# Products of depth 64 in pairs on the two halves of the array's rows

## The chip, the cores and the metric

One core of a Trainium2 chip runs the whole kernel as one program. The core has TensorE (PE in the rows; its weight loads are PEld), VectorE (DVE), ScalarE (ACT), GpSimd (POOL) and SyncE (SP), each with its own queue of instructions taken in order, and 16 DMA engines. The metric is the device time of the program in microseconds (us), median of three runs. Beside it stands one profiled execution, whose trace is read below.

## The reference

One encoder layer for 512 tokens of width 1024, in fp32: a mixer, a cross-attention into 256 memory tokens, a mixture of 64 experts (top 8 of them per token) with a shared expert, and a layer norm behind each. The change lies in the mixer. Its first group of heads is a sparse attention whose keys an indexer selects, its second a differential attention. What matters of it:

```python
# indexer: 8 heads of depth 64, one key of depth 64 for all heads, a weight per head and query
rel = jax.nn.relu(jnp.einsum('bqhd,bsd->bqhs', qib, k_idx) * IDX_DIM ** -0.5)
iscore = jnp.einsum('bqh,bqhs->bqs', wib, rel)          # then top 128 keys of each query
# sparse attention: queries of depth 64 go up to the latent of depth 128
q_lat = jnp.einsum('bqhd,hcd->bqhc', qb, w_uk)
sc = jnp.einsum('bqhc,bqkc->bqhk', q_lat, c_sel) * scale
# differential attention: 4 heads, two maps of depth 64 each
s1 = jnp.einsum('bqhd,bshd->bhqs', q1b, k1) * scale + bias
s2 = jnp.einsum('bqhd,bshd->bhqs', q2b, k2) * scale + bias
attn = softmax(s1) - lam * softmax(s2)
```

## The kernel before

**Numbers.** A product in fp32 is made of three in a rounded format: each operand is split into a high part (a cast on ScalarE) and a low part (source minus high, on VectorE or GpSimd; helper `split`, lines 94 and 95), and `mm3` (lines 101 to 103) adds high x high, high x low and low x high into one bank of PSUM. There are eight banks of 512 columns, handed out in turn by `bank()`; 20 large buffers (`slot`), 6 small ones (`wk`).

**Stages.** The layer norm and transposes of x; then the input projections, one block of 128 columns after the other (three products for each of 8 slices of the depth, 24 in all); the indexer's scores and the selection of 128 keys; the differential heads; the sparse attention; the memory attention; the router; then the experts, whose weights (3 x 1 MB each) stream in from HBM.

**Order.** Each part is a generator (`head_scores`, `index_scores`, `select`, `latent_up`, `dense` and so on) that issues a few instructions and yields two numbers: the time that its step takes on TensorE, and how long the next step isn't due. `schedule` holds a clock of its own, runs the first generator of a fixed list that is due, and so writes the program order of all engines before anything runs. `dense`, last in the list, goes through the projections and fills what the others leave; it yields after 12 products.

**The products of depth 64.** They are made in three ways. The differential heads (line 498) take the two maps of a head one after the other: the queries and keys of map 1 lie in partitions 0 to 63, those of map 2 in 64 to 127, and each map is an `mm3` of depth 64 with a yield behind it. The indexer (line 357) has two heads in the 128 partitions of a query tile; its key tile `kz` is held twice, once with zeros in the lower half and once with zeros in the upper, so that a product of depth 128 picks out one head. The sparse attention's way up to the latent (line 601) does the same with weights: `ukz` has zeros beside each head's 64 rows.

**The head weights of the indexer** (8 columns, 64 to 71 of the indexer's block) have a split of their own (`ww`) and a product of their own behind the key product (line 328), 24 products with 8 columns of weights over 384 tokens. The result goes through `wit` (line 330), three small transposes (line 334) and `widx`.

Of the kernel before, what the change touches and what calls it, by code (L numbers as in the profile page):

```python
# [11 lines left out]
F32R = mybir.dt.float32r  # L12
# [46 lines left out]
def encoder_layer(  # L59
# [245 lines left out]
    KW, IX = {}, {}  # L305

    def index_split(raw):
        hl = chunks.tile([P, 2, KD, P], F32R, tag="whl", name="kw", bufs=2)
        for j in range(2):
            js = slice(j * 64, (j + 1) * 64)  # L310
            split(hl[:, 0, :, js], hl[:, 1, :, js], raw[:, :, 0:64], lo_eng=nc.vector if j else nc.gpsimd)
        ww = wk([P, 2, KD, 8], F32R, name="ww")
        split(ww[:, 0], ww[:, 1], raw[:, :, 64:72])
        KW[0] = ww
        return hl

    def index_keys(wh, wl):
        ps = bank()
        yield from proj(ps, wh, wl, xt)
        kz = slot([P, 2, 2, SEQ], F32R, name="kz")  # L320
        IX["kz"] = kz
        fill0(kz[64:128, :, 0, :])
        fill0(kz[0:64, :, 1, :])
        for v in range(2):
            r = slice(64 * v, 64 * v + 64)
            split(kz[r, 0, v, :], kz[r, 1, v, :], ps[r, :])
        psw = bank()
        yield from proj(psw[0:8, 0:384], KW[0][:, 0], KW[0][:, 1], xt, P, SEQ)
        wit = wk([P, 384], name="wit")
        nc.scalar.activation(wit[0:8, :], psw[0:8, 0:384], AF.Copy, scale=float(A_HEADS) ** -0.5)  # L330
        yield 0.0, 0.0
        psw = bank()
        for i in range(3):
            nc.tensor.transpose(psw[:, i * 8:(i + 1) * 8], wit[0:8, i * P:(i + 1) * P], ident[0:8, 0:8])
# [13 lines left out]
    def index_scores():  # L348
        yield from wait("qi3")
        kz, qih, qil, widx = IX["kz"], IX[0], IX[1], IX["w"]  # L350
        for i in range(1, NT):
            w = (i + 1) * P
            isc = dsel[:, i - 1, :]
            q0 = (i - 1) * P
            for h in range(8):
                ps = bank()
                mm3(ps[:, 0:w], qih[:, h // 2, q0:q0 + P], qil[:, h // 2, q0:q0 + P],
                    kz[:, 0, h % 2, 0:w], kz[:, 1, h % 2, 0:w], True, True)
# [8 lines left out]
                yield 3 * w / 2400, w / 1500  # L367
# [118 lines left out]
    def head_scores():  # L486
        for h in range(B_HEADS):
# [47 lines left out]
    def latent_w():  # L535
        yield from wait("hs2")
        UW["uv"] = slot([P, 2, A_HEADS, P], F32R, name="uvz")
        UW["uk"] = slot([P, 2, A_HEADS, P], F32R, name="ukz")
        uvz, ukz = UW["uv"], UW["uk"]
# [4 lines left out]
        ukz_p = ukz.rearrange("p l (a v) c -> p l a v c", v=2)  # L544
# [5 lines left out]
        for l in range(2):  # L550
            fill0(ukz_p[64:128, l, :, 0, :])
            fill0(ukz_p[0:64, l, :, 1, :])
            fill0(uvz_p[:, l, :, 0, 64:128])
            fill0(uvz_p[:, l, :, 1, 0:64])
        yield 0.5, 1.0
        for v in range(2):
            r = slice(64 * v, 64 * v + 64)
            split(ukz_p[r, 0, :, v, :], ukz_p[r, 1, :, v, :], ps[r, :, :])
# [29 lines left out]
    def latent_up(u):  # L588

        us = slice(u * 256, (u + 1) * 256)  # L590
        for g in range(2):
            QL[u, g] = slot([P, 4, 2, 256], F32R, name="ql")
            for a in (2 * g, 2 * g + 1):
# [4 lines left out]
                for v in range(2):  # L598
                    h = 2 * a + v
                    ps = bank()  # L600
                    mm3(ps[:, 0:256], UW["uk"][:, 0, h, :], UW["uk"][:, 1, h, :], qa[:, 0, :], qa[:, 1, :], True, True)
                    split(QL[u, g][:, h % 4, 0, :], QL[u, g][:, h % 4, 1, :], ps[:, 0:256], scale=0.125 * 2.0 ** (h + 1))
                    yield 0.35, 0.2
# [1098 lines left out]
```

## Time and profile before

| | us |
|---|---|
| median of 3 runs (1312.59 to 1316.73) | 1313.4 |
| profiled execution, device time | 1301.79 |
| its span, first to last instruction | 1300.0 |
| TensorE busy, of the span | 1150.2 (88%) |
| weight loads busy | 907.3 (70%) |
| VectorE / ScalarE / GpSimd busy | 749.3 / 562.0 / 451.6 |

The profiled execution is one run; durations are read from it. Busy time is the union of an engine's instructions; matmuls overlap each other in the pipeline, so what one costs is the step from its start to the next one's start and not its duration. In the rows below, L12 is a line of the kernel, "out<-in" names the tiles, and a shape such as 64*128 64x512 is weights of 64 rows by 128 columns and a moving operand of 64 rows by 512 columns. An idle time names what ended it.

### The profile page before, as it was taken

How to read it: one execution, taken by the hardware profiler on the slowest of the kernel's cores; microseconds unless marked ns; L12 is line 12 of the kernel's file. 1: busy time of each engine (PE TensorE's matmuls, PEld its weight loads, DVE VectorE, ACT ScalarE, POOL GpSimd, SP SyncE). 2: the span in 40 equal slices, each digit the busy share in tenths (PEclk: the TensorE clock that was granted, in tenths of full speed). 3: DMA queues.
4: the chain of work that ended last, by engine and by line, in shares of the span. 5: the costliest groups of instructions: out<-in, count | busy, mean ns of one | idle time of the engine just before them, and what ended most of it. 6: DMA issues, size and time to landing. Idle time of an engine off the chain costs nothing. (4 is left out here: it accounts for less than half of the span.)

```text
span 1300.0 us, 20964 instructions
## 1 busy us (share of the span) xinstructions
PE 1150.2 (88%) x7768; PEld 907.3 (70%) x7768; DVE 749.3 (58%) x1602; ACT 562.0 (43%) x1006; POOL 451.6 (35%) x335
## 2 busy tenths in 40 slices
PE   2999999999898899879999999999879988898860
PEld 2887778998798798878877778777657544554320
DVE  7258986556865657787867777766456321311114
ACT  3235446654454443334645565555345112312122
POOL 4333444552236353461323322423222222222223
PEclk9999999999999899999999999999989998899895
DMA  7322134463426155688999999999999999999974
GB/s 224 82 81 65 49 99 117 123 206 122 130 65 211 50 175 204 229 306 301 294 316 332 349 327 356 339 355 360 349 331 342 342 345 377 380 360 363 356 272 141
DMA packets 136807, 319.37 MB, mean 246 GB/s; under 512 B 13296, under 2 KB 96240, under 8 KB 111872
## 3 DMA queue, kind: packets, MB, share of 16 engines
q1 hardware_dynamic: 119984, 275.83, 58.5%
q0 software_dynamic: 13632, 41.50, 13.7%
q8 instruction: 62, 1.02, 0.3%
q10 hardware_dynamic: 3088, 0.69, 0.3%
q14 instruction: 41, 0.34, 0.1%
HBM read 288.10 MB, written 35.19 MB: 249 GB/s over the span
## 5 line engine op out<-in xcount | busy, mean ns | idle before, releaser
L95 POOL TENSOR_TENSOR whl<-wraw,whl 128x1024 fp32r<-128x1024 f32 x81 | 195.6, 2416 | 265.4 <-ACT whl L94 239.4
L1357 POOL DMA_INDIRECT acc<-y,sidx x66 | 106.6, 1615 | 381.4 <-DMA acc<-y,sidx 205.9
L1269 DVE TENSOR_TENSOR whl<-wraw,whl 128x1024 fp32r<-128x1024 f32 x152 | 183.0, 1231 | 80.6 <-ACT whl L1268 80.0
L101 PE MATMUL ps<-whl,xt 128*96 128x256 f32 (+4 forms) x640 | 184.6, 288 | 3.9 <-ACT whl L1268 3.9
L102 PE MATMUL ps<-whl,xt 128*96 128x256 f32 (+4 forms) x640 | 179.8, 281 | 0.3 <-DVE whl L1269 0.3
L103 PE MATMUL ps<-whl,xt 128*96 128x256 f32 (+4 forms) x640 | 179.7, 281 | 0.0
L1268 ACT CAST whl<-wraw 128x1024 fp32r<-128x1024 f32 x152 | 152.3, 1054 | 25.3 <-DMA acc<-y,sidx 12.9
L1352 PE MATMUL ps<-wd,ht 128*96 128x512 f32 (+4 forms) x320 | 146.8, 602 | 3.2 <-DVE ht L1340 2.5
L1305 PE MATMUL ps<-wraw,xn 128*64 128x256 f32 (+1 forms) x832 | 114.8, 400 | 19.6 <-DMA wraw<-in_e_w_up_dram 7.7
L1324 ACT ACTIVATE sg<-ps 64x256 f32<-64x256 f32 (+6 forms) x66 | 25.0, 379 | 239.7 <-PE ps L1305 123.7
L94 ACT CAST whl<-wraw 128x1024 fp32r<-128x1024 f32 x91 | 95.4, 1048 | 57.5 <-PE ps L103 46.6
L1244 POOL DMA_INDIRECT xg<-rows,sidx x66 | 79.6, 1206 | 108.3 <-PE ps L1293 34.7
L101 PEld LDWEIGHTS ps<-whl,xt 128*96 128x96 f32 (+4 forms) x640 | 104.8, 164 | 4.6 <-ACT whl L1268 4.1
L102 PEld LDWEIGHTS ps<-whl,xt 128*96 128x96 f32 (+4 forms) x640 | 104.9, 164 | 0.7 <-DVE whl L1269 0.5
L103 PEld LDWEIGHTS ps<-whl,xt 128*96 128x96 f32 (+4 forms) x640 | 104.8, 164 | 0.3
L1305 PEld LDWEIGHTS ps<-wraw,xn 128*64 128x64 f32 (+1 forms) x832 | 60.0, 138 | 57.0 <-DMA wraw<-in_e_w_up_dram 9.7
L1352 PEld LDWEIGHTS ps<-wd,ht 128*96 128x96 f32 (+4 forms) x320 | 49.5, 163 | 71.2 <-issue 65.5
L1353 ACT COPY y<-ps 96x512 f32<-96x512 f32 (+4 forms) x80 | 46.4, 583 | 67.9 <-PE ps L1352 66.4
L1329 DVE SCALAR_TENSOR_TENSOR hm<-ps,og,sg 64x256 f32<-64x256 f32 (+4 forms) x54 | 36.8, 682 | 63.1 <-ACT sg L1324 51.0
L1340 DVE COPY ht<-ps 128x128 f32<-128x128 f32 (+6 forms) x66 | 21.5, 325 | 83.5 <-PE ps L1338 83.3
L101 PE MATMUL ps<-xTh,whl 128*128 128x512 f32 (+1 forms) x168 | 65.5, 390 | 0.0
L103 PE MATMUL ps<-xTh,whl 128*128 128x512 f32 (+1 forms) x168 | 63.8, 380 | 0.0
(421 smaller groups left out, 2763.4 us busy)
## 6 DMA issues: line engine op xcount, KB each, us to landing
wraw<-in_e_w_gate_dram SPq DMA_DIRECT2D x64, 1024.0 KB, 17.0
wraw<-in_e_w_up_dram SPq DMA_DIRECT2D x64, 1024.0 KB, 13.4
wd<-in_e_w_down_dram SPq DMA_DIRECT2D x64, 1024.0 KB, 13.3
wraw<-in_w_in_dram SPq DMA_DIRECT2D x21, 512.0 KB, 3.8
wraw<-in_m_wkv_dram SPq DMA_DIRECT2D x16, 512.0 KB, 4.4
wraw<-in_m_wq_dram SPq DMA_DIRECT2D x16, 512.0 KB, 4.0
wraw<-in_m_wo_dram SPq DMA_DIRECT2D x16, 512.0 KB, 3.5
wraw<-in_w_o_dram SPq DMA_DIRECT2D x12, 512.0 KB, 3.5
```

Of the source, the lines that this page charges most:

```text
L94: nc.scalar.copy(hi, src)
L95: eng.tensor_sub(lo, src, hi.bitcast(F32))
L101: nc.tensor.matmul(ps, lhsT=a, rhs=b, start=start, stop=False)
L102: nc.tensor.matmul(ps, lhsT=a, rhs=bl, start=False, stop=False)
L103: nc.tensor.matmul(ps, lhsT=al, rhs=b, start=False, stop=stop)
L1244: nc.gpsimd.indirect_dma_start(out=xg[0:n, :], out_offset=None, in_=rows, in_offset=bass.IndirectOffsetOnAxis(ap=gi[0:n, :], axis=0), boun ...
L1268: nc.scalar.copy(hi[v], w[i][v])
L1269: lo_eng.tensor_sub(lo[v], w[i][v], hi[v].bitcast(F32))
L1305: nc.tensor.matmul(ps[HALF * i:HALF * i + n, 0:256], lhsT=xt[:, k, 0:n], rhs=w[i][:, k, :], start=k == 0, stop=k == KD - 1)
L1352: nc.tensor.matmul(ps[0:n, :], lhsT=ht[:, j, 0:n], rhs=wd[:, j, cs], start=j == 0, stop=j == 1)
L1353: nc.scalar.copy(y[0:n, cs], ps[0:n, :])
L1357: nc.gpsimd.indirect_dma_start(out=acc, out_offset=bass.IndirectOffsetOnAxis(ap=si[0:n, :], axis=0), in_=y[0:n, :], in_offset=None, comput ...
```

## The change

Three edits put products of depth 64 side by side. A new helper takes two results and two sets of operands and issues their three products in turn, first of one half, then of the other:

```diff
+    def mm3_halves(pss, ops):
+        for i, j in ((0, 2), (0, 3), (1, 2)):
+            for ps, op in zip(pss, ops):
+                nc.tensor.matmul(ps, lhsT=op[i], rhs=op[j], start=i + j == 2, stop=i == 1)
+
+    HALVES = (slice(0, 64), slice(64, 128))
```

The differential heads use it for the two maps of a head, the indexer for two heads, the way up to the latent for two heads. The keys of the indexer are held once in each half (`kd`, the lower half filled by a DMA that GpSimd issues) instead of twice with zeros, and the way up has its weights once (`uk`) instead of twice with zeros:

```diff
@@ index_scores @@
-                ps = bank()
-                mm3(ps[:, 0:w], qih[:, h // 2, q0:q0 + P], qil[:, h // 2, q0:q0 + P],
-                    kz[:, 0, h % 2, 0:w], kz[:, 1, h % 2, 0:w], True, True)
+                if h % 2 == 0:
+                    pss = [bank()[:, 0:w] for _ in range(2)]
+                    mm3_halves(pss, [(qih[r, h // 2, qs], qil[r, h // 2, qs], kd[r, 0, 0:w], kd[r, 1, 0:w])
+                                     for r in HALVES])
+                ps = pss[h % 2]
...
-                yield 3 * w / 2400, w / 1500
+                if h % 2:
+                    yield 3 * w / 2400, 2 * w / 1500 + w / 1000
@@ head_scores @@
-                for v in range(2):
-                    r = slice(64 * v, 64 * v + 64)
-                    q = slice(i * P, (i + 1) * P)
-                    ps = bank()
-                    mm3(ps[:, 0:w], QK[h][r, 0, 0, q], QK[h][r, 0, 1, q], QK[h][r, 1, 0, 0:w], QK[h][r, 1, 1, 0:w],
-                        True, True)
+                q = slice(i * P, (i + 1) * P)
+                pss = [bank() for _ in range(2)]
+                mm3_halves([ps[:, 0:w] for ps in pss],
+                           [(QK[h][r, 0, 0, q], QK[h][r, 0, 1, q], QK[h][r, 1, 0, 0:w], QK[h][r, 1, 1, 0:w])
+                            for r in HALVES])
+                for v, ps in enumerate(pss):
                     t1 = at[:, OFF[i]:OFF[i + 1]] if v == 0 else wk([P, 512], name="t2")[:, 0:w]
                     pr.append((t1, soft(t1, ps, nd[:, 512 - w:512], w, sl)))
-                    yield 3 * w / 2400, w / 1000 + 0.1
+                yield 3 * w / 2400, 2 * w / 1000 + 0.2 + w / 800
@@ latent_up @@
-                for v in range(2):
+                pss = [bank()[:, 0:256] for _ in range(2)]
+                mm3_halves(pss, [(UW["uk"][r, 0, a, :], UW["uk"][r, 1, a, :], qa[r, 0, :], qa[r, 1, :]) for r in HALVES])
+                for v, ps in enumerate(pss):
                     h = 2 * a + v
-                    ps = bank()
-                    mm3(ps[:, 0:256], UW["uk"][:, 0, h, :], UW["uk"][:, 1, h, :], qa[:, 0, :], qa[:, 1, :], True, True)
...
-                    yield 0.35, 0.2
+                yield 0.35, 0.4
```

In `latent_w` the four clears and two splits of `ukz` give way to one split of `uk`. The fourth edit is in `index_keys`: the key product takes 72 columns of weights, and the last 8 rows of its result are the head weights:

```diff
-        yield from proj(ps, wh, wl, xt)
-        kz = slot([P, 2, 2, SEQ], F32R, name="kz")
-        fill0(kz[64:128, :, 0, :])
-        fill0(kz[0:64, :, 1, :])
-        for v in range(2):
-            r = slice(64 * v, 64 * v + 64)
-            split(kz[r, 0, v, :], kz[r, 1, v, :], ps[r, :])
-        psw = bank()
-        yield from proj(psw[0:8, 0:384], KW[0][:, 0], KW[0][:, 1], xt, P, SEQ)
+        yield from proj(ps[0:72, :], wh[:, :, 0:72], wl[:, :, 0:72], xt)
+        kd = slot([P, 2, SEQ], F32R, name="kd")
+        split(kd[0:64, 0, :], kd[0:64, 1, :], ps[0:64, :])
+        nc.gpsimd.dma_start(kd[64:128, :, :], kd[0:64, :, :])
         wit = wk([P, 384], name="wit")
-        nc.scalar.activation(wit[0:8, :], psw[0:8, 0:384], AF.Copy, scale=float(A_HEADS) ** -0.5)
+        nc.scalar.activation(wit[64:72, :], ps[64:72, P:SEQ], AF.Copy, scale=float(A_HEADS) ** -0.5)
```

With new products and new yields `schedule` writes another order. Line numbers of the changed kernel are its own: its 109 is the product in `mm3_halves`. TensorE at the last score block of a differential head (qk its queries and keys, kz and qi those of the indexer, xT and whl a projection; numbers are buffers), before:

```order
L103 MATMUL ps_961<-xTh_144,whl_850 128x512
L101 MATMUL ps_1044<-qk_744 128x512
L102 MATMUL ps_1044<-qk_744 128x512
L103 MATMUL ps_1044<-qk_744 128x512
L101 MATMUL ps_1054<-kz_305,qi_345 128x512
L102 MATMUL ps_1054<-kz_305,qi_345 128x512
L103 MATMUL ps_1054<-kz_305,qi_346 128x512
L101 MATMUL ps_1061<-qk_744 128x512
```

The same block after:

```order
L103 MATMUL ps_1106<-xTh_143,whl_1039 128x512
L109 MATMUL ps_1119<-qk_796 128x512
L109 MATMUL ps_1120<-qk_796 128x512
L109 MATMUL ps_1119<-qk_796 128x512
L109 MATMUL ps_1120<-qk_796 128x512
L109 MATMUL ps_1119<-qk_796 128x512
L109 MATMUL ps_1120<-qk_796 128x512
L101 MATMUL ps_1106<-xTh_144,whl_1039 128x512
```

The two maps stood apart with other work between them and now stand interleaved, into two banks; the index scores, which ran beside the first head, now end before it. Of such pairs there are 16 of the heads, 12 of the indexer and 8 of the way up, each between products of depth 128.

ScalarE from the last transposes of x to the head weights, before:

```order
L94 CAST xTh<-ps 128x4x128 x4
L94 CAST kz<-ps 64x512
L94 CAST whl<-wraw 128x1024
L94 CAST kz<-ps 64x512
L330 ACTIVATE wit<-ps 8x384
```

And after:

```order
L94 CAST xTh<-ps 128x4x128 x4
L94 CAST kd<-ps 64x512
L94 CAST whl<-wraw 128x1024
L330 ACTIVATE wit<-ps 8x384
L94 CAST qi<-ps 128x384
```

One of the two key casts goes; wit stays behind the cast of the next weights.

VectorE just ahead of the first head score (line 393, at and t its maps; 378 and 379 are a round of the selection on dsel, 365 a weighted index score), before:

```order
L378 MAX m_1313<-dsel 128x8
L379 MATCH_REPLACE dsel<-m_1313,dsel 128x256
L381 TENSOR_SCALAR dsel<-dsel 128x256
L365 SCALAR_TENSOR_TENSOR dsel<-rl,widx,dsel 128x384
L382 TENSOR_TENSOR dsel<-dsel 128x256
L365 SCALAR_TENSOR_TENSOR dsel<-rl,widx,dsel 128x384
L393 ISA at,m_872<-ps,dsel 128x128
```

And after (381 and 382 are the round, 396 the head score):

```order
L382 MATCH_REPLACE dsel<-m_1642,dsel 128x384
L381 MAX m_1707<-dsel 128x8
L382 MATCH_REPLACE dsel<-m_1707,dsel 128x384
L381 MAX m_1751<-dsel 128x8
L396 ISA at,m_929<-ps,dsel 128x128
L396 ISA m_929 128x1
L396 ISA t_935,m_936<-ps,dsel 128x128
```

Before the first head score VectorE used to have all of the first selection and 14 of the 24 index scores; now it has all 24 scores, the first selection and 14 of the 16 rounds of the second (and the start of a fifteenth). In TensorE's order, 14 half projections of 12 products stand between the first index pair and the first head pair.

## Rows read from the trace of the kernel before

**Rows 1.** Stretch, length; PE, PEld, DVE, ACT, POOL busy (count); clock, DMA share, GB/s

```profile
62.20:109.80 47.60, 47.08 (x231) 39.58 (x229) 31.38 (x71) 18.97 (x33) 19.98 (x10) 1.00 0.30 80
109.80:249.00 139.20, 132.07 (x726) 106.64 (x726) 109.28 (x289) 76.99 (x165) 59.66 (x32) 1.00 0.31 88
249.00:620.00 371.00, 339.94 (x2555) 319.56 (x2554) 249.94 (x530) 172.33 (x331) 154.86 (x105) 0.97 0.54 182
620.00:950.00 330.00, 315.22 (x2184) 248.73 (x2182) 222.81 (x398) 177.93 (x268) 99.93 (x76) 0.99 1.00 338
950.00:1262.00 312.00, 277.35 (x1888) 160.33 (x1888) 89.93 (x228) 87.83 (x168) 77.04 (x63) 0.95 0.99 352
```

**Rows 2.** Waits of SyncE's queue: us in total, times, longest

```profile
SPq L1251 <- DMA acc<-y,sidx: 210.0, 17, 17.6
```

**Rows 3.** Timeline of TensorE around one head score (start us, us, instruction)

```profile
183.99 0.39 PE L103 MATMUL ps<-xTh,whl 128*128 128x512 f32 x1
184.30 0.50 PE L101 MATMUL ps<-qk 64*128 64x512 f32 x1
184.64 0.39 PE L102 MATMUL ps<-qk 64*128 64x512 f32 x1
184.88 0.39 PE L103 MATMUL ps<-qk 64*128 64x512 f32 x1
185.19 0.50 PE L101 MATMUL ps<-xTh,whl 128*128 128x512 f32 x1
185.53 0.39 PE L102 MATMUL ps<-xTl,whl 128*128 128x512 f32 x1
```

**Rows 4.** Timeline of TensorE, steps of 384 and of 256 columns

```profile
43.00 0.34 PE L102 MATMUL ps<-xTl,whl 128*128 128x384 f32 x1
43.18 0.34 PE L103 MATMUL ps<-xTh,whl 128*128 128x384 f32 x1
...
62.23 0.28 PE L101 MATMUL ps<-kz,qi 128*128 128x256 f32 x1
62.35 0.28 PE L102 MATMUL ps<-kz,qi 128*128 128x256 f32 x1
```

**Rows 5.** First of each tile's three lines: count, ns min/median/max, first and last start, shapes

```profile
L101 PE MATMUL ps<-qk x32: 322/412/497, 109.8 to 247.5; 64*128 64x128 f32 x8, 64*128 64x256 f32 x8, 64*128 64x384 f32 x8, 64*128 64x512 f32 x8
...
L101 PE MATMUL ps<-kz,qi x24: 277/348/500, 62.2 to 136.1; 128*128 128x256 f32 x8, 128*128 128x384 f32 x8, 128*128 128x512 f32 x8
...
L101 PE MATMUL ps<-qa,ukz x16: 279/283/415, 254.7 to 326.2; 128*128 128x256 f32 x16
...
L101 PE MATMUL ps<-xTh,ww x8: 332/336/522, 31.1 to 41.2; 128*8 128x384 f32 x8
```

**Rows 6.** Timeline of TensorE: expert products, unpaired (L1352) and in column halves (L1316)

```profile
699.61 3.17 PE L1352 MATMUL ps<-wd,ht 128*112 128x512 f32 x7
...
1023.71 1.89 PE L1316 MATMUL ps<-wd,ht 128*64 128x512 f32 x8
```

**Rows 7.** Timeline of ScalarE behind the key product

```profile
37.92 0.58 ACT L94 CAST kz<-ps 64x512 fp32r<-64x512 f32 x1 [6.58 <-PE ps L103]
38.41 1.05 ACT L94 CAST whl<-wraw 128x1024 fp32r<-128x1024 f32 x1
...
41.91 0.48 ACT L330 ACTIVATE wit<-ps 8x384 f32<-8x384 f32 x1 [1.84 <-PE ps L103]
```

**Rows 8.** Timeline of GpSimd in the same stretch

```profile
39.53 2.40 POOL L95 TENSOR_TENSOR whl<-wraw,whl 128x1024 fp32r<-128x1024 f32 x1 [11.39 <-ACT whl L94]
```

**Rows 9.** VectorE, 50 to 260 us, by shape: busy us, mean ns, idle before

```profile
L365 DVE SCALAR_TENSOR_TENSOR dsel<-rl,widx,dsel 128x384 f32<-128x384 f32 x7 | 10.1, 1443 | 0.0
...
L378 DVE MAX8 m<-dsel 128x8 f32<-128x384 f32 x16 | 8.8, 552 | 0.3
L379 DVE MATCH_REPLACE8 dsel<-m,dsel 128x384 f32<-128x384 f32 x16 | 8.7, 542 | 0.0
...
L365 DVE SCALAR_TENSOR_TENSOR dsel<-rl,widx,dsel 128x512 f32<-128x512 f32 x7 | 6.2, 882 | 0.0
```

More of the change, by code (lines that the diff above doesn't have):

```diff
@@ L302, in ln_in @@
         nc.vector.memset(nd[0:64, 448:512], NEG)
-    KW, IX = {}, {}
+    IX = {}
     def index_split(raw):
         hl = chunks.tile([P, 2, KD, P], F32R, tag="whl", name="kw", bufs=2)
[L309 to L314, printed above, removed]
+        for k in (slice(0, 4), slice(4, 8)):
+            split(hl[:, 0, k, 0:72], hl[:, 1, k, 0:72], raw[:, k, :])
         return hl
@@ L318, in index_keys @@
         ps = bank()
[L319 to L328 removed]
+        yield from proj(ps[0:72, :], wh[:, :, 0:72], wl[:, :, 0:72], xt)
+        kd = slot([P, 2, SEQ], F32R, name="kd")
+        IX["k"] = kd
+        split(kd[0:64, 0, :], kd[0:64, 1, :], ps[0:64, :])
+        nc.gpsimd.dma_start(kd[64:128, :, :], kd[0:64, :, :])
         wit = wk([P, 384], name="wit")
[L330 removed]
+        nc.scalar.activation(wit[64:72, :], ps[64:72, P:SEQ], AF.Copy, scale=float(A_HEADS) ** -0.5)
         yield 0.0, 0.0
@@ L333, in index_keys @@
         for i in range(3):
-            nc.tensor.transpose(psw[:, i * 8:(i + 1) * 8], wit[0:8, i * P:(i + 1) * P], ident[0:8, 0:8])
+            nc.tensor.transpose(psw[:, i * 8:(i + 1) * 8], wit[64:72, i * P:(i + 1) * P], ident[64:72, 64:72])
         widx = small.tile([P, 3, 8], F32, name="widx", bufs=1)
@@ L349, in index_scores @@
         yield from wait("qi3")
-        kz, qih, qil, widx = IX["kz"], IX[0], IX[1], IX["w"]
+        kd, qih, qil, widx = IX["k"], IX[0], IX[1], IX["w"]
         for i in range(1, NT):
@@ L353, in index_scores @@
             isc = dsel[:, i - 1, :]
-            q0 = (i - 1) * P
+            qs = slice((i - 1) * P, i * P)
             for h in range(8):
-                ps = bank()
-                mm3(ps[:, 0:w], qih[:, h // 2, q0:q0 + P], qil[:, h // 2, q0:q0 + P],
-                    kz[:, 0, h % 2, 0:w], kz[:, 1, h % 2, 0:w], True, True)
+                if h % 2 == 0:
[3 more added lines that the diff above has]
+                ps = pss[h % 2]
                 rl = wk([P, 512], name="rl")
@@ L537, in latent_w @@
         UW["uv"] = slot([P, 2, A_HEADS, P], F32R, name="uvz")
-        UW["uk"] = slot([P, 2, A_HEADS, P], F32R, name="ukz")
-        uvz, ukz = UW["uv"], UW["uk"]
+        UW["uk"] = slot([P, 2, 4, P], F32R, name="uk")
+        uvz, uk = UW["uv"], UW["uk"]
         ukr = wk([P, A_HEADS, 64], name="ukr")
@@ L543, in latent_w @@
         nc.scalar.dma_start(uvr, a_w_uv[0].rearrange("h c d -> c h d"))
-        ukz_p = ukz.rearrange("p l (a v) c -> p l a v c", v=2)
         uvz_p = uvz.rearrange("p l (a v) c -> p l a v c", v=2)
@@ L555, in latent_w @@
         yield 0.5, 1.0
+        split(uk[:, 0], uk[:, 1], ps)
         for v in range(2):
             r = slice(64 * v, 64 * v + 64)
-            split(ukz_p[r, 0, :, v, :], ukz_p[r, 1, :, v, :], ps[r, :, :])
             split(uvz_p[:, 0, :, v, r], uvz_p[:, 1, :, v, r], uvr_p[:, :, v, :])
@@ L597, in latent_up @@
                 yield 0.0, 0.8
-                for v in range(2):
+                pss = [bank()[:, 0:256] for _ in range(2)]
+                mm3_halves(pss, [(UW["uk"][r, 0, a, :], UW["uk"][r, 1, a, :], qa[r, 0, :], qa[r, 1, :]) for r in HALVES])
+                for v, ps in enumerate(pss):
                     h = 2 * a + v
-                    ps = bank()
-                    mm3(ps[:, 0:256], UW["uk"][:, 0, h, :], UW["uk"][:, 1, h, :], qa[:, 0, :], qa[:, 1, :], True, True)
-                    split(QL[u, g][:, h % 4, 0, :], QL[u, g][:, h % 4, 1, :], ps[:, 0:256], scale=0.125 * 2.0 ** (h + 1))
-                    yield 0.35, 0.2
+                    split(QL[u, g][:, h % 4, 0, :], QL[u, g][:, h % 4, 1, :], ps, scale=0.125 * 2.0 ** (h + 1))
+                yield 0.35, 0.4
     PA = {}
```

2 lines of the change are left out of this document (removed).

## The prediction

> **What bounds the kernel now.** I read the busy time of the engines in stretches first, then the timeline of TensorE at the products that change, then their counts, last VectorE in the stretch where the work is rearranged. Up to 620 us TensorE does the work of the mixer, the memory attention and the shared expert and hardly rests: in 62 to 249 us, where the index scores and the head scores run, it is busy 179.2 of 186.8 us, in 249 to 620 us 339.9 of 371 [rows 1]. The DMA engines are half idle there. From 620 us on the expert weights keep them busy the whole time, and TensorE stays at 315 of 330 us; from 950 us TensorE has slack (277 of 312) and the stream of weights sets the pace. SyncE's queue tells how that stage is paced: its loads wait 210 us in total, in 17 waits, for the scatter that frees a buffer [rows 2], so a load follows the block that went before it and not a clock of its own. The stage hangs as a whole on the moment at which the front ends, and from there the program order after the change is the same (the tail of 2704 rows of TensorE's order is equal). So each microsecond that leaves TensorE before 620 us should leave the end, as long as no new idle time takes its place. VectorE is the engine to watch: 109.3 of 139.2 us in 110 to 249 us.
>
> **What a switch of depth costs.** In the trace a head's three products of depth 64 stand alone between products of depth 128. From the start of the last product ahead of them (183.99) to the start of the second one behind them (185.53) there are five steps, 1.54 us. A step of 512 columns inside one kind is 0.23 to 0.24 (184.64 to 184.88), five are 1.15. The trio thus pays 0.39 beyond its columns, about half going in and half coming out [rows 3]. The Trainium skill, "TensorEngine Tiling (Array Packing)", section Key Properties, says that a change of tiling mode drains the engine while a change of tile alone does not; the first half is what this row shows. The rule speaks against two of the three edits: index scores and latent queries have no such switch now and get one.
>
> **Steps by width.** A 256-wide step is 0.12 (62.23 to 62.35), a 384-wide one 0.18 (43.00 to 43.18) [rows 4]. I take 0.12 for 128 columns too.
>
> **Do two halves overlap?** No row shows two products in the two halves of the rows side by side. The nearest are the narrow experts, whose products stand in pairs in the two halves of the columns: 8 of 512 columns (4 pairs) last 1.89 us from first start to last end, while 7 unpaired ones last 3.17. With a step g and a last duration d, 3g+d=1.89 and 6g+d=3.17 give g=0.43 for a pair and for a single one alike [rows 6]. A pair costs what one costs. That is my value for rows too, with no overlap at all as the other end. The weight loads of a pair are the term between: if these went one after another, a pair of any width would take at least 2 x 0.12.
>
> **Head scores.** 96 products, 24 of each width (32 rows on each of three lines, eight of each width [rows 5]): 24 x (0.23+0.18+0.12+0.12) = 15.6 us of columns and 32 trios x 0.39 = 12.5 of switches, 28.1 in all. After: 7.8 + 16 pairs x 0.39 = 14.0. Gain 14.1. Nearly half of it is switches saved, which does not hang on overlap.
>
> **Index scores.** 72 products: 24 x (0.23+0.18+0.12) = 12.7 now, without a switch. After: 6.4 + 12 x 0.39 = 11.1. Gain 1.6; without overlap a loss of 4.7.
>
> **Latent queries.** 48 of 256 columns: 5.8 now; after 2.9 + 8 x 0.39 = 6.0. Loss 0.2; without overlap 3.1.
>
> **Head weights of the indexer.** 24 products of 384 columns go, 24 x 0.18 = 4.3 us. But they covered something: behind the key product ScalarE takes kz (0.58, from 37.92), the next weight tile (1.05), and only then wit, which now starts at 41.91, once the head-weight product is done [rows 7]. With the weights in the key product, wit can start at 37.92+0.58+1.05 = 39.55, 2.36 us earlier than now, and TensorE stands idle meanwhile, since the transposes of wit are next in its queue. Gain 2.4, not 4.3.
>
> **The copy of the keys.** POOL now issues a DMA for the lower half, behind one weight split and ahead of six. It waits for the low part of the keys (37.92 + 0.58 on ScalarE and, as an estimate, as much on VectorE behind it, 39.1), and the split queued behind it takes 2.40 [rows 8] and is wanted when the first query product ends, about 40.3 + 24 x 0.18 = 44.6. No row shows an issue of this kind; up to 2.5 us of it would still fit, so I take nothing, with 1 us as the other end. The copy itself has until the first index score; the four query products before it take 24 x 0.18 us each.
>
> **Clears and splits.** Four clears of ukz and two of kz leave VectorE, and half of the key splits. They stand where VectorE has room; I count nothing, and at most 2 us if they now hold up a transpose.
>
> **The sum.** 14.1 + 1.6 - 0.2 + 2.4 = 17.9 us of TensorE. Against it stands VectorE. By the order, from the first index score to the first head score it now gets 14 more rounds of the second selection (0.55+0.54 each, 15.3), 7 more weighted sums of 512 (0.88, 6.2) and 2 of 384 (1.44, 2.9) [rows 9]: 31.4 [rows 1] + 24.4 = 56 us. TensorE has 11.1 of pairs, 14 half projections of 12 x 0.23 = 38.6 and 12 small products there, 51 us. VectorE falls some 5 us behind. Spare banks and result buffers take up some of that, and over both stretches it has 140.7 us [rows 1] for about 169 us, so it catches up. I take 4 us of new waits on TensorE. **Forecast: 14 us less.** The profiled execution took 1301.8 us (span 1300.0), so it would become 1287.8. The timed runs lie 11.6 us above it, at a median of 1313.4; nothing in the change depends on that distance, so the prediction is 1313.4 - 14 = 1299.4 us.
>
> **Rivals.**
> 1. VectorE becomes the bound. For it: 79% busy in 110 to 249 us, and both score maps of a pair now come at once. If the 5 us are lost in full and each of the 16 head pairs waits 0.5 us more, 13 are lost: 4.9 less, 1308.5. Against it: the selection rounds that fill VectorE are wanted only much later.
> 2. The weight loads of a pair go one after another. Then every pair step of up to 512 columns costs 0.24: heads 12 x 4 x 0.24 = 11.5 rather than 7.8, index 8.6 rather than 6.4, latent 5.8 rather than 2.9, 8.8 less gain: 14 - 8.8 = 5 less, 1308. For it: loads and products of 256 columns have the same step now. The Trainium skill, "TensorE: Matmul & The Clock Gate", section Measured speedup vs the span model, has 3.07 rather than 4 for four row tiles; a partial overlap of that size would, as an estimate, cost 5 us of the gain. No run here shows it.
> 3. The change doesn't do what it says: no overlap of row halves. 14.1 becomes 6.3, 1.6 becomes -4.7, -0.2 becomes -3.1, with 2.4 that is 0.9, and VectorE isn't pressed: 1312.5.
> 4. Slower: going from the upper to the lower half costs a switch as going to depth 64 does. A pair has five such steps of about 0.2, 36 pairs have 180 of them, 36 us; on top of rival 3, 35 more, 1348. It decides from 18 us on, that is from 0.1 us per step. Against it: the column pairs change halves at each product and show none of it.
>
> **Chances.** Forecast 0.60, VectorE 0.14, loads in turn 0.10, no overlap 0.08, switches between halves or the like 0.08. The forecast's own range, with 0 to 9 us of waits and the small terms, is 1294 to 1305; rivals 1 and 2 take the range to 1310, and if VectorE costs nothing and the clears give their 2 us, 1292. A measurement of this kernel can tell 0.3%, 4 us. Faster: 0.60 + most of 0.14 + over half of 0.10 = 0.78; within: 0.12; slower: 0.10.
>
> **What will show it.** The six products of a pair should stand in three twos, both starts of a two a few ns apart, and 512-wide twos 0.23 apart; starts in single file mean rival 3, twos of 256 columns 0.24 apart rival 2. The switch should still be 0.39 per pair. wit should start near 39.5 and the first query product near 40.3. TensorE's idle time between the first index score and the last head score tells what VectorE took; over about 20 us there means rival 1. The last head score should come earlier by more than the sum, since the order puts projections off behind it, and the first router product 14 us earlier. From there both traces should run in step; if the lead is lost behind 620 us, my first paragraph is wrong.

## The result, and the profile after

The changed kernel takes 1301.2 us (median of 22 runs) and the kernel before, run beside it, 1308.0 (22 runs): a ratio of 0.9949, 95% interval 0.9928 to 0.997. It is 6.8 us faster; 14 were forecast. The profiled execution took 1297.9 us, its span is 1296.0:

```profile
core 0: 1296.0 us, clock 0.954
```

The mean clock is lower than before (0.962 for a span of 1300.0), and the two spans are 4.0 us apart, less than the medians. The five stretches again, to set beside [rows 1] (stretch, length; busy time of PE, PEld, DVE, ACT, POOL; clock, DMA share, GB/s):

```profile
62.20:109.80 47.60, 47.30 (x238) 35.07 (x238) 39.54 (x93) 21.02 (x40) 17.64 (x9) 1.00 0.26 69
109.80:249.00 139.20, 123.88 (x729) 101.66 (x727) 98.76 (x273) 73.47 (x165) 62.92 (x32) 0.95 0.31 86
249.00:620.00 371.00, 342.51 (x2568) 321.15 (x2566) 251.06 (x523) 171.20 (x326) 155.32 (x104) 0.96 0.57 188
620.00:950.00 330.00, 318.77 (x2179) 248.99 (x2178) 222.05 (x402) 178.95 (x269) 102.52 (x75) 0.98 1.00 339
950.00:1262.00 312.00, 270.44 (x1867) 157.92 (x1865) 85.13 (x218) 84.19 (x163) 78.69 (x64) 0.95 0.98 345
```

The change shows in the second row: TensorE was busy 132.07 us there and is now busy 123.88, with the clock at 0.95 where it was 1.00. VectorE has moved forward: 39.54 us in the first row where it had 31.38, and 98.76 in the second where it had 109.28.

One pair of head scores with its neighbours, to set beside the trio of [rows 3] (start, us, instruction):

```profile
174.22 0.95 PE L423 MATMUL ps<-mean_c,sq 128*128 128x1 f32 x8
175.09 0.96 PE L109 MATMUL ps<-qk 64*128 64x512 f32 x6
175.98 0.65 PE L484 MATMUL ps<-ident,vt 128*128 128x128 f32 x4
176.39 0.48 PE L101 MATMUL ps<-xTh,whl 128*128 128x512 f32 x1
```

The view puts the six products into one row. From the first of them to the next instruction are 175.98 - 175.09 = 0.89 us, and one trio alone took 185.19 - 184.30 = 0.89 before. The six starts behind the row are 175.091 and .094, 175.426 and .428, 175.655 and .658: three twos, 2 to 3 ns apart, 0.23 us between the last two. Medians of the time from a group's first start to the next instruction, trio before and pair after: 0.546 and 0.553 at 256 columns, 0.718 and 0.725 at 384, 0.889 and 0.892 at 512. Two products in the two halves cost what one costs.

The head weights on ScalarE and TensorE ([rows 7]), and the copy of the keys on GpSimd ([rows 8]):

```profile
39.42 0.58 ACT L94 CAST kd<-ps 64x512 fp32r<-64x512 f32 x1 [8.51 <-PE ps L103]
39.90 1.04 ACT L94 CAST whl<-wraw 128x1024 fp32r<-128x1024 f32 x1
40.97 0.48 ACT L330 ACTIVATE wit<-ps 8x384 f32<-8x384 f32 x1
```

```profile
38.99 0.40 PE L103 MATMUL ps<-xTh,kw 128*72 128x512 f32 x1
41.51 0.35 PE L334 MATMUL ps<-ident,wit 8*128 8x8 f32 x3 [2.12 <-ACT wit L330]
```

```profile
41.04 0.79 POOL L328 DMA_DIRECT2D kd<-kd  x1 [13.98 <-DVE kd L95]
41.85 2.41 POOL L95 TENSOR_TENSOR whl<-wraw,whl 128x1024 fp32r<-128x1024 f32 x1
```

wit follows the weight cast directly, as worked out, and TensorE stands idle 2.12 us for it (0.57 before). The issue of the copy takes 0.79 us, and the weight split behind it ends at 44.3, in time.

What TensorE waits for between 28 and 592 us (us in total, times, longest), the first lines of after. Here `whl` is the split weights of a projection, `ukr` the latent weights as loaded, `maskb` the router's mask and `qk` a head's queries and keys; further down `vt` is a head's values, `at` its score maps and `memh` the memory tokens:

```profile
PE ps L103 <- POOL whl L95: 8.3, 8, 1.7
PE ps L102 <- POOL whl L95: 5.0, 4, 2.8
PE ps L551 <- DMA ukr<-in_a_w_uk_dram: 3.9, 1, 3.9
PE ps L1050 <- DVE maskb L1039: 2.4, 1, 2.4
PE ps L109 <- POOL qk L412: 2.3, 1, 2.3
```

Before, the wait for maskb is 2.4 us too; the second line has 2.0 there, those of qk and ukr 1.7 and 1.2, and the first reads:

```profile
PE ps L103 <- POOL whl L95: 2.4, 3, 1.1
```

For all kernels below I use five numbers. **Experts** is the time at which TensorE starts on the first transposes of the experts, in the one profile. **Idle** is the sum of TensorE's idle time up to there. **Front** is the clock's loss in the same stretch: its length times one minus its mean clock. **Clock** is the same loss over the whole span, as a mean over the timed runs, and **rest** is the mean time less that: what a run would take at full clock, if every lost cycle counted.

| kernel | median us | ratio to before | experts | idle | front | clock | rest |
|---|---|---|---|---|---|---|---|
| before | 1308.3 | 1 | 597.0 | 61.2 | 11.9 | 54.0 | 1254.0 |
| changed | 1301.2 | 0.9949 | 591.4 | 67.8 | 20.5 | 60.2 | 1241.0 |
| heads_only | 1307.8 | 0.9986 | 607.7 | 75.1 | 22.2 | 57.3 | 1250.5 |
| rest_only | 1326.4 | 1.0131 | 610.5 | 66.4 | 25.6 | 66.6 | 1258.1 |
| pads | 1301.5 | 0.9971 | 594.7 | 70.0 | 18.8 | 59.1 | 1243.8 |
| trios | 1299.1 | 0.9934 | 596.6 | 68.3 | 23.9 | 58.6 | 1240.3 |
| filler | 1297.3 | 0.9920 | 591.1 | 62.4 | 20.5 | 54.8 | 1243.4 |
| one_half | 1301.4 | 0.9957 | 589.3 | 58.8 | 10.2 | 54.3 | 1248.2 |
| pace | 1293.8 | 0.9911 | 582.8 | 66.2 | 11.9 | 56.4 | 1237.6 |
| pace_vt | 1297.3 | 0.9908 | 590.7 | 67.8 | 18.8 | 58.9 | 1237.8 |
| pace_head | 1292.0 | 0.9889 | 583.6 | 66.8 | 11.9 | 56.2 | 1236.3 |
| sel_late | 1298.5 | 0.9949 | 591.9 | 66.4 | 20.5 | 57.9 | 1242.0 |

(before: the 74 runs beside the experiments. The standard error of the rest is 0.4 to 2.0 us. One run of filler, of 3016 us, is left out.) Experts, idle and front are of one execution each. Those of rest_only, pace and pace_head are the fastest runs of their kernels, 6 to 12 us under the median.

The first two rows already say most: if every lost cycle counts, the changed kernel is 13.0 us faster at full clock, and 6.2 of these go to a lower clock. The profiles show the same work gone: without idle time and clock loss the way to the experts takes 597.0 - 61.2 - 11.9 = 523.9 us before and 591.4 - 67.8 - 20.5 = 503.1 after.

### The profile page after: what moved, and what is told of

It is laid out like the page before. It is cut to its first block, busy times and chain, and to the rows that moved or that the text cites. A ratio compares the mean times of both kernels' runs of the same rounds, so it can differ in the third digit from the quotient of the medians.

```text
span 1296.0 us, 20931 instructions
## 1 busy us (share of the span) xinstructions
PE 1139.9 (88%) x7744; PEld 895.3 (69%) x7744; DVE 739.2 (57%) x1594; ACT 555.8 (43%) x1003; POOL 456.3 (35%) x335
## 3 DMA queue, kind: packets, MB, share of 16 engines
q1 hardware_dynamic: 119984, 275.83, 58.8%
## 5 line engine op out<-in xcount | busy, mean ns | idle before, releaser
L1352 PE MATMUL ps<-wd,ht 128*96 128x512 f32 (+4 forms) x320 | 147.6, 604 | 4.0 <-DVE ht L1340 3.1
L1352 PEld LDWEIGHTS ps<-wd,ht 128*96 128x96 f32 (+4 forms) x320 | 49.6, 164 | 72.7 <-issue 66.1
L103 PE MATMUL ps<-xTh,whl 128*128 128x512 f32 (+1 forms) x168 | 65.1, 387 | 3.7 <-POOL whl L95 3.7
L101 PE MATMUL ps<-xTh,whl 128*128 128x512 f32 (+1 forms) x168 | 67.9, 404 | 0.3 <-ACT whl L94 0.3
```

What stands on the lines that cost most here:

```text
L1352: nc.tensor.matmul(ps[0:n, :], lhsT=ht[:, j, 0:n], rhs=wd[:, j, cs], start=j == 0, stop=j == 1)
```

## The experiments

**The two kernels again.** No edit; a second profile of each.

> The kernel before, profiled once more, to see whether what separates the two traces repeats. Theory 1 (waits and clock: TensorE saves the 17.9 us of the sum, and most of it comes back as waits of TensorE for GpSimd, ScalarE and one DMA, and as stretches of half clock behind such waits): up to the first expert transposes about 61 us of idle time on TensorE and 6 stretches of half clock again, within 3 us and one stretch. Rival A (the difference between the two profiles is chance of one execution): idle time or stretches differ from the first profile by more than 6 us or two stretches.

> The changed kernel, profiled once more. Theory 1: the waits of over 1 us at the same places (wit 2.1, first head pair 2.3, first transposes of values 2.0, weight splits at 131 to 149 us 3.7 in all, transposes of the latent weights 3.9), about 68 us idle in front of the experts, 6 or 7 stretches of half clock, first expert transposes near 591 us. Rival A: waits or stretches at other places.

before_again took 1304.6 us, with 62.0 us idle and 10.2 lost to the clock in front, as expected; after_again 1303.0, with 70.2 and 27.3. Three waits stand at the same places (wit 2.12, qk 2.32, ukr 3.70). These belong to the kernel and not to one execution. The rest of the expectation for after_again failed: the wait for vt is 0.44 us instead of 2.00, two waits for whl of 1.92 and 2.16 us stand where there were three of 1.44, 1.26 and 1.03, the front has 11 stretches at half clock instead of 6, and the experts start at 599.9 us and not near 591.

**One part alone.** heads_only is the kernel before with the pairs in the head scores; rest_only is the changed kernel without them.

```
-                for v in range(2): ... mm3(ps[:, 0:w], QK[h][r, 0, 0, q], ...)
-                    yield 3 * w / 2400, w / 1000 + 0.1
+                mm3_halves([ps[:, 0:w] for ps in pss], [... for r in HALVES])
+                yield 3 * w / 2400, 2 * w / 1000 + 0.2 + w / 800
```

> The kernel before with the head scores alone in pairs; index scores, way up to the latent and head weights as before. TensorE's sum: 14.1 us less. Theory 1: the pairs step as in the changed kernel (two starts a few ns apart, 0.39 for the switch), and again part of the 14.1 comes back in waits: 4 to 10 us faster than before, 1298 to 1304 beside 1308. Rival B (VectorE is the bound between the first index score and the last head score): the index scores keep their pace, so less is lost there than in the full change, and nearly the whole 14 stay: 12 to 14 us faster.

> The changed kernel with the head scores as before (two trios with a yield behind each); index scores and way up in pairs, head weights in the key product. TensorE's sum: 1.6 - 0.2 + 2.4 = 3.8 us less. Theory 1: 0 to 4 us faster than before, with the wait for wit of 2 us in its trace. Rival B: the index scores' pairs crowd VectorE, so slower than before by 0 to 4 us.

heads_only: ratio 0.9986 (0.996 to 1.0013), no change where the theories had 4 to 10 and 12 to 14 us less: its idle time rises by 13.9 us, about what the pairs save. rest_only: 1.0131 (1.0091 to 1.0171), 17 us slower, which neither theory had. The products go as in the sum: without idle time and clock loss the way to the experts is 13.5 and 5.4 us shorter than before, where the sum has 14.1 and 1.6 - 0.2 + 4.3 = 5.7. But at full clock the parts come to -3.5 and +4.1 us, both together to -13.0. The times do not add up, and most of rest_only's loss is clock (66.6 against 54.0). Each edit also moves the order in which the planner puts projections between the scores; that this is what costs rest_only its time is not shown.

**More distance at the waits.**

```
+            if n == 0: ... transposes of wit, widx      (behind the first query product)
+            yield 0.0, 2.5                              (head_scores, behind wait k)
-            yield 0.0, 0.6                              (head_vt)
+            yield 0.0, 2.0
+        yield 0.0, 5.0                                  (latent_w, before the ukr transposes)
```

> Edit: the changed kernel, with the three places that TensorE waits at put further from what they wait for: the small transposes of the index weights (wit) behind the first index query product, 2.5 us of pause after a head's keys and before its first scores, 2 instead of 0.6 us before the transposes of the head values, 5 us before the transposes of ukr. The work is the same. Theory 1 (half of the saving went into new waits of TensorE for GpSimd, ScalarE and a DMA, and into the half clock that follows them): idle time of TensorE up to the first expert transposes falls from 67.8 to 62 us or less, the waits of 2.12 (wit), 2.32 (qk), 2.00 (vt) and 3.88 us (ukr) are gone or under 1 us, the loss by the granted clock there falls from 20.5 towards 12; time 1288 to 1296, ratio to the kernel before 0.985 to 0.99. Rival (VectorE has become the bound, so a wait taken away at one place comes back at another): idle 66 to 69, time as in the changed kernel, ratio 0.993 to 0.997.

Ratio 0.9971 (0.9948 to 0.9994), idle 70.0. The waits for wit, qk and ukr are gone, and others have come: `vt` 2.15 us (at 147.3 us), `at` 3.58 (156.6), `memh` 1.80 (198.1). The expectation of theory 1 fell; the rival's numbers (66 to 69 us, 0.993 to 0.997) are missed by a hair, and its case is what the trace shows.

**The same six products, half by half.**

```
-        for i, j in ((0, 2), (0, 3), (1, 2)):
-            for ps, op in zip(pss, ops):
+        for ps, op in zip(pss, ops):
+            for i, j in ((0, 2), (0, 3), (1, 2)):
```

> Edit: the changed kernel, with the six products of a pair written as a trio of one half and then a trio of the other, so that no two neighbours lie in different halves except at the one switch; order of all other work as in the changed kernel. Overlap theory: the twos that start 3 to 4 ns apart are gone, a pair takes two steps more (four saved steps are three now two more than after: about 5.2 us in the head scores, 4.2 in the index scores, 1.9 in the latent queries, 11 together); at full clock that is 1241 + 11 = 1252, measured about +8 to +17 against the changed kernel, ratio to the kernel before 0.999 to 1.007. Rival (the pairs gain nothing by overlap, what moved the time was the other order of the work): the same time as the changed kernel within 2 us, ratio 0.993 to 0.997.

Ratio 0.9934 (0.9912 to 0.9955), as the changed kernel. This would look like a point for the rival, but the trace shows another reason (trios, the same place):

```profile
175.22 0.97 PE L109 MATMUL ps<-qk 64*128 64x512 f32 x6
176.12 0.66 PE L484 MATMUL ps<-ident,vt 128*128 128x128 f32 x4
```

0.90 us, as in the changed kernel: the starts still come in twos, now 8 to 10 ns apart. The expected two extra steps were never there. The products need not alternate for the overlap; two trios that are neighbours are enough.

**No overlap, same order.** To take the overlap away without moving anything, both trios use the same half; the second map or head of each pair is left out and the first made twice. So the experts get other tokens, and what that does to the time behind is not shown.

```
-            for ps, op in zip(pss, ops):
+            for ps, op in zip(pss, (ops[0], ops[0])):
```

> Edit: the changed kernel, with the second trio of every pair taken from the same half of the rows as the first (so the second product of a pair repeats the first one's factors: head, index and latent query scores of every second head or component are not those of the reference). The order of all instructions, their shapes and their number are as in the changed kernel; only the halves are not both used. Overlap theory (the two halves work side by side, and that alone saves the steps): no two of a pair's products start within 10 ns of each other; three steps more for each pair: head scores 16 pairs, 4 x 3 x (0.23 + 0.17 + 0.12 + 0.11) = 7.6 us, index scores 8 x 3 x (0.23 + 0.17 + 0.12) = 12.5 us (24 pairs), latent queries 16 x 3 x 0.12 = 5.8 us, 26 us in all of TensorE's time; the time 15 to 26 us above the changed kernel, ratio to the kernel before 1.006 to 1.016. Rival (the gain of the changed kernel lies in the order of its instructions and in fewer of them, not in the overlap): within 3 us of the changed kernel, ratio 0.992 to 0.998.

(The expected 26 us counts twice as many index and latent pairs as there are; with 12 and 8 it is 16.7.) The trace has the extra steps:

```profile
175.27 1.65 PE L109 MATMUL ps<-qk 64*128 64x512 f32 x6
176.85 0.66 PE L484 MATMUL ps<-ident,vt 128*128 128x128 f32 x4
```

1.58 us instead of 0.89. Summed by width over all pairs the overlap is worth 16.6 us of TensorE. Yet the time is 1301.4, ratio 0.9957 (0.9925 to 0.999): the same as with overlap. The table shows where the 16.6 go. The changed kernel has 9.0 us more idle time than one_half, which leaves 7.6, and at full clock it is 7.2 faster (1248.2 - 1241.0); 5.9 of these it loses again by its clock (60.2 against 54.3). one_half waits for wit, qk and ukr as the changed kernel does (2.1, 2.2 and 4.0 us), so these waits do not come from the overlap. It has no wait for vt, and the first line of the list above is half as high:

```profile
PE ps L103 <- POOL whl L95: 4.4, 5, 1.7
```

**Whose waits are they?** The chain behind the wait at 128 us in the changed kernel, ScalarE and then TensorE:

```profile
126.14 0.40 ACT L399 ACTIVATE at<-at,m 128x128 f32<-128x128 f32 x1 [13.10 <-DVE m L396]
...
127.26 0.56 ACT L473 COPY vt<-ps 128x512 f32<-128x512 f32 x1
127.73 1.04 ACT L94 CAST whl<-wraw 128x1024 fp32r<-128x1024 f32 x1
```

```profile
127.88 0.66 PE L484 MATMUL ps<-ident,vt 128*128 128x128 f32 x4 [2.00 <-ACT vt L473]
...
131.49 0.80 PE L103 MATMUL ps<-xTh,whl 128*128 128x512 f32 x1 [1.44 <-POOL whl L95]
132.08 0.63 PE L101 MATMUL ps<-xTh,whl 128*128 128x512 f32 x1
132.51 0.63 PE L102 MATMUL ps<-xTl,whl 128*128 128x512 f32 x1
```

Read it upwards: TensorE waits for ScalarE and GpSimd, GpSimd's split needs ScalarE's cast, and ScalarE had stood 13.10 us at the first exponential, for VectorE, which was in its selection rounds. The views name the last link alone. So sel_late holds the second and third selection back behind the first two heads; TensorE's order does not move.

```
-            nc.vector.memset(isc[0:64, w - 64:w], -1e38)          (index scores, i = 2, 3)
+                nc.vector.tensor_scalar(dsel[0:64, h + 1, w - 64:w], at[0:64, 1216:1280], 0.0, -1e38,
+                                        op0=OP.mult, op1=OP.add)   (end of head h = 0, 1)
```

> Edit: the changed kernel, with the second and third selections of the 128 largest index scores (32 rounds of MAX8 and MATCH_REPLACE8 on VectorE, 0.56 + 0.54 us at 384 columns and 0.68 + 0.68 at 512) held back behind the first and the second head's scores: the small write that every selection starts from now reads a value of that head. TensorE's order is the same, the work is the same (one 64x64 write in another form). VectorE theory: VectorE is full from 80 to 165 us, ScalarE's exponentials of the first head scores wait 13.1 us for it, and behind them in ScalarE's queue stand the copy of the head values (vt) and the next weight split, so that TensorE's waits for vt (2.00) and whl (1.44, 1.26, 1.03) between 127 and 150 us are VectorE's. Then these waits are under 0.6 us each, ScalarE's waits for L396 between 100 and 190 us fall from 36.2 to under 20 us, idle time up to the first expert transposes falls from 67.8 to 60 to 63 us, and the time falls 5 to 10 us under the changed kernel, to 1291 to 1297, ratio to the kernel before 0.986 to 0.992. Rival (the waits are GpSimd's and ScalarE's own, or come back elsewhere when taken away, as in pads): idle 66 to 70 us, time as in the changed kernel, ratio 0.993 to 0.997.

Stretches of the changed kernel, and the same three of sel_late:

```profile
106.00:165.00 59.00, 50.66 (x228) 37.78 (x227) 58.07 (x143) 22.21 (x49) 24.17 (x12) 0.94 0.21 55
165.00:206.00 41.00, 40.44 (x248) 33.77 (x247) 22.21 (x76) 29.29 (x67) 20.37 (x12) 1.00 0.33 102
206.00:222.00 16.00, 11.96 (x80) 10.87 (x80) 6.54 (x22) 7.35 (x17) 5.58 (x5) 0.79 0.50 123
```

```profile
106.00:165.00 59.00, 56.69 (x271) 44.66 (x272) 34.93 (x109) 30.80 (x69) 28.06 (x15) 0.97 0.26 72
165.00:206.00 41.00, 37.05 (x223) 30.86 (x221) 35.75 (x107) 23.16 (x51) 17.79 (x11) 0.96 0.28 85
206.00:222.00 16.00, 10.98 (x76) 10.16 (x76) 15.13 (x32) 5.80 (x15) 5.08 (x3) 0.89 0.41 106
```

The first exponential in sel_late, to set beside the 13.10 us above:

```profile
117.64 0.40 ACT L400 ACTIVATE at<-at,m 128x128 f32<-128x128 f32 x1 [4.01 <-DVE m L397]
```

The first row decides the cause: VectorE (the third busy time) falls from 58.07 of 59 us to 34.93, and TensorE rises from 50.66 to 56.69; its waits of over 0.9 us between 125 and 185 us are gone. They were VectorE's. But VectorE is now busy 70.6 of the 77 us from 145 to 222, and from 189 us on TensorE waits again (vt 1.23, memh 1.89, whl 1.93). ScalarE's wait for VectorE is 28.2 us and not under 20. Idle time 66.4, ratio 0.9949 (0.9921 to 0.9978): the cause was right, the expected gain did not come.

**The clock.** filler puts 14 products nobody reads into the wait for ukr.

```
+        pd = bank("pd")
+        for k in range(14):
+            nc.tensor.matmul(pd, lhsT=xt[0][0][:, 0, 0:P], rhs=xt[0][0][:, k % 4, :], start=k == 0, stop=k == 13)
```

> Edit: the changed kernel, with 14 products of 512 columns that nobody reads put right before the transposes of ukr, where TensorE waits 3.9 us for a DMA; they take 14 x 0.23 = 3.2 us at full clock. Theory 1 (a wait of TensorE of 2 us or more is what its clock falls behind): the wait is filled, the stretch at half clock at about 211 us is gone, and the time falls by the clock that comes back, 1 to 4 us under the changed kernel. Rival (the stretches at half clock come whatever stands there): the stretch at about 211 us stays, the time stays or rises by up to 3 us.

```profile
209.60 3.45 PE L551 MATMUL pd<-xTh 128*128 128x512 f32 x14
213.65 0.63 PE L554 MATMUL ps<-ident,ukr 128*128 128x128 f32 x4 [0.60 <-DMA ukr<-in_a_w_uk_dram]
```

```profile
206.00:222.00 16.00, 15.23 (x115) 13.59 (x114) 7.53 (x27) 8.88 (x23) 7.72 (x5) 1.00 0.50 123
```

Beside the 0.79 of the changed kernel above, the clock is 1.00: the stretch at half clock is gone with the wait. The median falls by 3.9 us to 1297.3, ratio 0.992 (0.9894 to 0.9946); that interval overlaps the changed kernel's, so the gain is likely but not settled. In the one profile the whole front loses as much clock as in the changed kernel's (20.5 us), since stretches of 3.4 us at half clock stand at 43 and 118 us that are not in the other; the mean over the runs is 54.8 against 60.2.

**The order alone.** pace gives the planner the costs of before (head and index), pace_head those of the heads alone, pace_vt is pace with 2.0 us before the vt transposes.

```
-                yield 3 * w / 2400, 2 * w / 1000 + 0.2 + w / 800
+                yield 6 * w / 2400, 2 * w / 1000 + 0.2
```

> Edit: the changed kernel with the costs that the head and index scores tell the planner put back to the sum of the two halves in the kernel before (6w/2400 of TensorE and 2w/1000 + 0.2 of pause for a pair of head scores, 6w/2400 and 2w/1500 for a pair of index scores, in place of 3w/2400 and a pause longer by w/800 and w/1000); the products and their pairs are as in the changed kernel, the order in which they stand among the projections moves. Theory 1 takes the saving of TensorE as given and the rest as waits: last head score 5 to 15 us earlier or later than 234 us, but the front end's work is the same; if the order hardly matters, within 4 us of the changed kernel (ratio 0.992 to 0.998). Rival (the order in which the planner puts projections between the scores is worth as much as the products): idle time of TensorE up to the first expert transposes 73 us or more, time 6 us or more above the changed kernel, ratio 1.000 or more.

> Edit: the changed kernel with the cost of a pair of head scores alone put back to the sum of before (6w/2400 of TensorE, 2w/1000 + 0.2 of pause); index scores tell the planner what they tell it in the changed kernel. If the earlier head scores are what made pace faster (last head score at 222.5 instead of 234.2 us there): last head score 220 to 226 us, time as pace, ratio 0.988 to 0.994. Rival (pace is faster by the index scores' part of the order, or by both together only): as the changed kernel, ratio 0.993 to 0.997.

> Edit: the kernel pace, with 2.0 instead of 0.6 us of pause before the transposes of the head values, which wait 4.98 us for ScalarE there at 127.4 us. Theory (waits of TensorE can be taken away one by one): that wait is under 1 us, idle time up to the first expert transposes falls from 66.2 to 61 to 63 us, time 2 to 5 us under pace, ratio 0.986 to 0.989. Rival (a pause moves the order of everything behind it, and a wait as long turns up elsewhere, as in pads): idle 64 to 70 us, time within 4 us of pace on either side, ratio 0.989 to 0.995.

pace: 0.9911 (0.988 to 0.9942), just outside the first expectation and far from the rival's, since the order mattered in the other direction. pace_head: 0.9889 (0.9857 to 0.9921), last head score at 223.2 as expected; **it has the lowest median, 1292.0 us**, with the same products as the changed kernel; pace and pace_vt lie within its interval. In its profile TensorE does not wait for ukr at all, and the clock stays up there:

```profile
206.00:222.00 16.00, 16.00 (x132) 14.96 (x132) 13.54 (x42) 14.39 (x36) 8.66 (x4) 1.00 0.46 124
```

It gains 4.0 us of clock and 4.7 at full clock against the changed kernel. The first fits its missing wait; where the second comes from is open, since its idle time (66.8) is hardly lower. In the one profile, which is of its fastest run, the time behind the start of the experts is 700.4 us against 704.6. pace_vt removed the vt wait and got whl 1.72, 2.16, 1.05 and ukr 2.77 in its place: 0.9908 (0.9883 to 0.9932), the rival's case again.

## Why the forecast was half right

- **The number: luck.** 1299.4 us were forecast and 1301.2 measured, but two errors cancel. The forecast set out from 1313.4, the median of three runs, where 22 runs have 1308.0; and its gain of 14 us is twice the 6.8 that came (3.9 to 9.4 by the interval of the ratio).
- **Overlap and switch: right.** A pair costs what a trio cost, and one_half prices the overlap at 16.6 us where the sum's terms hold 17.0 (7.8 + 6.3 + 2.9). Rivals 2, 3 and 4 fall as mechanisms: the last twos of 256 columns are 0.12 apart, and nothing drains between the halves. For rival 2 the prediction named the Trainium skill's "TensorE: Matmul & The Clock Gate", section Measured speedup vs the span model, with 3.07 for four row tiles; two halves here show 2 x 0.889 / 0.892 = 1.99, without such a loss. No run here has four.
- **Head weights: right.** In this pair of profiles wit starts only 0.94 us earlier than before, not 2.36, because the key product itself ends 1.5 later (37.92 to 39.42); in the other kernels with this edit the end lies between 36.9 and 39.6. Over the eleven profiles with the edit wit starts at 39.9 us in the mean (38.5 to 41.2), over the three without at 42.1, which is 2.2 earlier. Behind the key product the three steps of ScalarE are as worked out.
- **The stage behind stays in step: right.** From the first expert transposes to the end of the span it takes 700 to 708 us in all 14 profiles. SyncE's waits for the scatter remain its pace (184.8 us in 17 waits, [rows 2]).
- **The step that failed: "I take 4 us of new waits on TensorE".** VectorE does fall behind where the prediction put it, but three things were wrong. The size: 6.6 us more idle time than before, and 9.0 more than the same order without overlap. The length: "it catches up" counted VectorE's total over both stretches, while ScalarE's queue feels the block in which VectorE is full, 106 to 165 us: 58.07 of 59 us, where it was 54.85 before and 55.83 in one_half:

```profile
106.00:165.00 59.00, 54.66 (x253) 41.76 (x252) 54.85 (x139) 29.62 (x62) 20.75 (x11) 1.00 0.21 58
```

```profile
106.00:165.00 59.00, 56.78 (x252) 44.33 (x252) 55.83 (x150) 28.38 (x61) 23.52 (x12) 0.97 0.27 71
```

  ScalarE's wait for VectorE between 100 and 190 us doubles, here before, after and in one_half:

```profile
ACT at L396 <- DVE m L393: 18.3, 6, 4.8
```

```profile
ACT at L399 <- DVE m L396: 36.2, 9, 13.1
```

```profile
ACT at L399 <- DVE m L396: 21.3, 8, 4.7
```

  And the price: a wait was counted at its own length, with no term for the clock, which by the table took 6.2 us more. Rival 1 had the right engine and a nearer number (4.9 less), by half a microsecond at each head pair, which no trace shows.
- **The account.** The 17.9 us of the sum have the head weights at 2.4, their 4.3 us of products less a wait that is part of the idle time here; products alone are 19.8. Less 6.6 of idle time that is 13.2; at full clock the runs give 13.0, and 6.8 are left behind the clock. The profiles show how much of this belongs to one execution. In the first pair the work in front falls by 20.8 us, idle time and clock loss rise by 6.6 and 8.6, and the experts start 5.6 us earlier (597.0 to 591.4). In the second pair it is 22.9, 8.2 and 17.1, and they start 2.4 us later (597.5 to 599.9). (Idle time at half clock counts twice in this, so the work comes out a little high.) Where in the run the 6.8 us of the medians are won, the two pairs do not tell.
- **"The first router product 14 us earlier": wrong**, it came 0.4 later (522.4 to 522.8; 1.5 later in the second pair). The last head score came 14.3 us earlier, not more than the sum, and the lead was gone by the end of the first mixer (last product of oTh at 420.5, 420.3 before): the projections put off behind the heads (80 products more stand behind the last head score), with their waits and half clock, took it. Most of the 5.6 us at the experts arose only behind 578 us: before waits 2.62 us for VectorE at 584.7 and then runs at half clock. The changed kernel's first profile has no such wait there, its second has 2.11 us at 587.6.
- **Rival 3's price was wrong too.** A kernel without overlap was put at 0.9 us less than before; one_half is 7 us less. By the account above it has 19.8 - 16.6 = 3.2 us of products and 2.4 of idle time less than before, 5.6 us; at full clock the runs give 5.8.

## What to carry over

When an engine that seems to be the bound gets faster, look for the stretch in which the next engine is full and count what is queued behind its waits; a mean over a stage hides it. Follow a wait back by its chain, since the view names the last link alone. And price an edit together with the order that it brings: here the order alone, with the products unchanged, moved the time more (pace_head, 8 to 9 us by ratio or median) than the overlap did (one_half, about 1 us).

## What the hardware showed that I had not expected

- Two trios in different halves of the rows run side by side even when they are issued one after the other (trios: starts 8 to 10 ns apart, 0.90 us for six products). By these starts the first product of the second trio begins ahead of two that stand before it in the kernel. How near two trios must stand for it no run shows; those of before, with other work between them, did not overlap.
- The granted clock falls to its lower level (1.2 of 2.4 GHz) in waits of TensorE or right behind them; in front of the experts the profiles have it there for 3.4 to 10.2 us at a time. In the changed kernel it falls behind the wait of 2.00 us for vt, and in the rows at 132 us above a step of 512 columns is 0.43 us instead of 0.23. The wait for ukr is 2.8 to 4.1 us in seven of the 14 profiles, and each of these has such a stretch in it or behind it; in the other seven it is 2.1 us or less or is not there, and none has. Not each wait is followed: of ten profiles with the 2.12 us for wit, seven have a stretch behind it, the changed kernel's first one not.
- Over the 22 runs of the changed kernel the time goes with the clock's loss (correlation 0.78, 0.94 us for each us lost), over the 74 of before less closely (0.68, and 0.64 us). The 6.2 us of clock in the table are thus, as an estimate from these two slopes, 4 to 6 us of time.
